# A four-layer hybrid decoder trunk: order of scores and values in the cross attention, the convolution's parameters on another queue, and later issue of norm scales and of the split memory

## The chip, the cores and the metric

The kernel runs on one core of one Trainium2 chip, as one program. The metric is the device time of that program in microseconds. Three runs of the kernel before gave 2044.0 to 2047.51 us, with a median of 2045.81. The profile shows one further execution, of 2043.62 us.

The core's engines each work through their own instructions in order: TensorE (PE in the profile, with PEld for its weight loads), VectorE (DVE), ScalarE (ACT), GpSimd (POOL) and SyncE (SP), which here only issues transfers. ScalarE and GpSimd have queues for transfers too, and an issue stands in line with their other instructions.

## The reference

The input is x of 256 tokens with 1024 features, and a memory of 256 tokens. There are four layers; each has a token mixer, a cross attention into the memory and an MLP. After each of these three the residual stream is normalized:

```python
for i in range(DEPTH):                     # 4 layers
    kind, j = i % N_MIXERS, i // N_MIXERS  # conv, dilated attention, RWKV-7, conv
    ...                                    # h = the token mixer of x
    x = layer_norm(DEEPNORM_ALPHA * x + h, ln_g[i, 0], ln_b[i, 0])
    h = memory_cross_attention(x, mem, x_w_q[i], x_w_kv[i], x_w_out[i])
    x = layer_norm(DEEPNORM_ALPHA * x + h, ln_g[i, 1], ln_b[i, 1])
    h = sq_relu_mlp(x, m_w1[i], m_w2[i])
    x = layer_norm(DEEPNORM_ALPHA * x + h, ln_g[i, 2], ln_b[i, 2])
```

The two parts that the change touches are these:

```python
def conv_module(x, w_in, b_in, dw, dw_b, ln_g, ln_b, w_out, b_out):
    h = x @ w_in + b_in
    val, gate = jnp.split(h, 2, axis=-1)
    h = val * jax.nn.sigmoid(gate)
    h = lax.conv_general_dilated(h, dw[:, None, :], ...) + dw_b   # causal, 31 taps, one filter a feature
    h = jax.nn.silu(layer_norm(h, ln_g, ln_b))
    return h @ w_out + b_out

def memory_cross_attention(x, mem, w_q, w_kv, w_out):             # 4 heads of 256
    q = (x @ w_q).reshape(b, s, XATTN_HEADS, XATTN_HEAD_DIM)
    kv = (mem @ w_kv).reshape(b, mem.shape[1], 2, XATTN_HEADS, XATTN_HEAD_DIM)
    p = jax.nn.softmax(jnp.einsum('bshe,bmhe->bhsm', q, kv[:, :, 0]) * (XATTN_HEAD_DIM ** -0.5), axis=-1)
    o = jnp.einsum('bhsm,bmhe->bshe', p, kv[:, :, 1])
    return o.reshape(b, s, D_MODEL) @ w_out
```

## The kernel before

**Products.** Every large product is computed from split operands: a matrix is a high part in a short format plus the low rest, and three matmuls (high by high, high by low, low by high) are summed in PSUM. Weights come in pieces of 128 x 1024 numbers (512 KB) through `chunk` (L131 to L141): SyncE issues the load into a staging tile `ws` (three buffers), ScalarE casts it to `wh` (L139), and an engine subtracts to get `wl` (L140; nine buffers each of `wh` and `wl`). That engine is VectorE in most of the kernel, and GpSimd (`lo_eng`) in the convolution's first part. A staging buffer is free when the subtraction has read it. x is transposed by TensorE and split in the same way into `xth` and `xtl` (`to_xt`, L153 and L154).

**Order.** The program is written as Python code that names the work; a scheduler with costs of its own then sets the order of each engine's instructions, near the order in which the code names them, and gives out the buffers. A transfer that is named late can therefore still be issued early, if its buffer is free and its queue has nothing else that can go.

**The convolution (layers 0 and 3).** `conv` loads the layer's norm scales (`load_gb`: `lng` and `lnb`, each a row spread to 128 partitions, 512 KB written), then the parameters (`conv_cols`): filter taps, biases and the inner norm's scales lie as rows, are loaded in three parts into one tile `craw` (one buffer, L465, L468, L470), transposed by TensorE (L471) and copied into `ccols` (L472). Then three tracks are merged by a table of due times: `glu` (eight units of 48 matmuls each, gate and value by turns, in PSUM tiles `psB` of which there are two), the taps on VectorE (L536), and the keys and values of the memory (`kv_unit`, units of 48 matmuls too). A gate unit ends in a sigmoid on ScalarE (L495), a value unit in an addition of its bias (L503); both read `ccols`.

**The memory.** In layer 0 `mem_t` loads the memory into `memrow` (which shares its buffer with `lng`), transposes and splits it into `mt`, and writes both parts to DRAM as `memd` (two writes of 1 MB, L305). Later layers read them back by GpSimd's queue (L297).

**The cross attention.** `xattn` computes q for 128 tokens at a time, in two banks of PSUM of 512 features, that is two heads, each (`first_rows`). A bank is copied (L381), transposed (L214) and copied into the four tiles of the heads (L384). `scores` of a head does eight fp32 matmuls on TensorE (four named ones of two passes, L346), the maximum on VectorE (L350, L351), the exponential on ScalarE (L355) and the division (L356, L359). `values` transposes the result, copies it by ScalarE (L366), multiplies it with the memory's values (L370) and splits the outcome into `oxt`. `project` then multiplies `oxt` with the output weights and normalizes. PSUM tiles `psA`, of which there are four, hold q's banks, the scores and the projection's sums.

Of the kernel before, what the change touches and what calls it, by code (L numbers as in the profile page):

```python
# [11 lines left out]
F32 = mybir.dt.float32  # L12
# [7 lines left out]
P = 128  # L20
# [64 lines left out]
class Trunk:  # L85
# [113 lines left out]
    def first_rows(self, xt, t, ws):  # L199


        out = [self.A(), self.A()]
        if t == 0:
            self.gemm_tok(xt, t, ws, out)
        else:
            for j in range(2):
                self.gemm_tok(xt, t, [[a[:, j * 512:(j + 1) * 512] for a in w] for w in ws], out[j:j + 1])
        return out
# [83 lines left out]
    def mem_t(self, tags=("xth", "xtl")):  # L292

        mt = [self.sb.tile([P, KC, S], F32R, name="mt", tag=g, bufs=2) for g in tags]
        if self.mem_d is not None:
            for a, d in zip(mt, self.mem_d):
                self.nc.gpsimd.dma_start(a, d)  # L297
            return mt
        for m in range(NT):
            mm = self.sb.tile([P, D], F32, name="memrow", tag="lng", bufs=1)  # L300
            self.nc.sync.dma_start(mm, self.t["mem"][0, m * P:(m + 1) * P, :])
            self.to_xt(mt, mm, m)
        self.mem_d = [self.dr.tile([P, KC, S], F32, name=f"memd{i}") for i in range(2)]
        for a, d in zip(mt, self.mem_d):
            self.nc.sync.dma_start(d, a.bitcast(F32))  # L305
        return mt
# [25 lines left out]
    def xattn(self, layer, kv, xt, xt_out):  # L332
# [52 lines left out]
        scores(0)  # L385
        scores(1)
        values(0)
        scores(2)
        values(1)
        scores(3)  # L390
# [64 lines left out]
    def conv_cols(self, j, cp):  # L455
# [3 lines left out]
        pt = self.T()  # L459
        dw = t_["a_dw"][j].rearrange("w (c p) -> (w c) p", p=P)  # L460
        for q in range(3):
            raw = cp.tile([P, P], F32, name="craw", tag="craw", bufs=1)
            if q < 2:
                n = 124
                nc.sync.dma_start(raw[:n, :], dw[q * n:(q + 1) * n, :])  # L465
            else:
                n = 40
                nc.sync.dma_start(raw[:16, :], t_["a_b_in"][j].rearrange("(c p) -> c p", p=P))  # L468
                for i, nm in enumerate(("a_dw_b", "a_ln_g", "a_ln_b")):
                    nc.sync.dma_start(raw[16 + 8 * i:24 + 8 * i, :], t_[nm][j].rearrange("(c p) -> c p", p=P))  # L470
# [6 lines left out]
    def conv(self, layer, j, xt, xt_out, fill):  # L477

        nc, v, t_ = self.nc, self.nc.vector, self.t
        gb = self.load_gb(layer, 0)  # L480
# [112 lines left out]
        self.lo_eng = v  # L593
        boh, bol = self.chunk(t_["a_b_out"][j:j + 1, :], None, rows=1)
# [712 lines left out]
def tile_trunk(ctx: ExitStack, tc: tile.TileContext, t: dict, out: bass.AP, stop: int = 99, layers=tuple(range(DEPTH))):  # L1307
# [12 lines left out]
    def memory(ls, tags):  # L1320
# [4 lines left out]
        return [lambda l=l, u=u: k.kv_unit(l, kv[l], u, mt) for l in ls for u in range(8)]  # L1325
# [94 lines left out]
```

## Time and profile before

| | |
|---|---|
| median of three runs | 2045.81 us |
| the profiled execution | 2043.62 us, its span 2041.9 us |
| TensorE busy | 1933.6 us, 95% of the span |
| VectorE, ScalarE, GpSimd busy | 1294.5, 994.7 and 270.4 us |
| transfers | 334.14 MB, 164 GB/s over the span |
| layer 0's convolution | from the start to about 184 us |
| the four cross attentions, from the end of q's last bank to the end of the values | 233 to 254, 799 to 819, 1366 to 1387 and 1801 to 1824 us |

Matmuls follow each other in a pipeline, so a record's duration (some 280 ns for 128 x 256) is longer than the time from one to the next (120 ns). Idle time of TensorE is therefore read from the stretches without any of its work, and the granted clock (1.00 or 0.50 in any short stretch) is looked at beside it.

### The profile page before, as it was taken

The numbers are of one execution on the slowest core, as the hardware profiler recorded it, in microseconds if no ns is written. First come the engines' busy times: TensorE is split into PE (matmuls) and PEld (weight loads), VectorE is DVE, ScalarE is ACT, GpSimd is POOL, SyncE is SP. The second block draws the span as 40 slices with busy tenths as digits, with TensorE's granted clock in tenths as the row PEclk, the third lists the DMA queues.
The fourth block names the chain that finished last, engine by engine and source line by source line (L and its number), as shares of the span: only waits on it lengthen the run. The fifth ranks groups of instructions, "written<-read, shape, count | busy, mean of one in ns | idle before, by whom it ended". The sixth has DMA issues, their size and how long they took to land.

```text
span 2041.9 us, 32951 instructions
## 1 busy us (share of the span) xinstructions
PE 1933.6 (95%) x12995; PEld 1708.8 (84%) x12995; DVE 1294.5 (63%) x2516; ACT 994.7 (49%) x1543; POOL 270.4 (13%) x168
## 2 busy tenths in 40 slices
PE   6999989999999998999999989989999898999998
PEld 6998779888999987798888777867898787878996
DVE  3896755546555566655496668776554599756544
ACT  4545536544545544365436544433655464545552
POOL 5870000000000000000021312100001653000000
PEclk8999999999999999999999889989999999999999
DMA  7644547667565645376645333553665532435762
GB/s 248 198 156 137 175 148 234 188 186 204 167 174 160 176 136 163 112 227 194 193 127 162 115 91 119 191 181 121 209 193 178 166 125 72 150 109 183 217 188 73
DMA packets 260604, 334.14 MB, mean 164 GB/s; under 512 B 25798, under 2 KB 220062, under 8 KB 259169
## 3 DMA queue, kind: packets, MB, share of 16 engines
q1 hardware_dynamic: 258144, 322.59, 51.2%
q0 software_dynamic: 1152, 8.39, 1.2%
q8 instruction: 102, 1.67, 0.3%
q10 hardware_dynamic: 1152, 1.05, 0.2%
q14 instruction: 54, 0.43, 0.1%
HBM read 321.96 MB, written 8.98 MB: 162 GB/s over the span
## 4 chain that ended last, share of the span: by engine, by line
PE 70%; DVE 14%; DMA 6%; ACT 4%; issue 4%; POOL 2%; SPq 0%; DVEq 0%; ACTq 0%; POOLq 0%
PE psA L172 25%; PE psB L184 19%; PE psB L196 7%; PE psB L655 6%; DVE g L536 3%; PE psT L214 3%; DVE wl L140 2%; ACT wh L139 2%; DMA ws<-in_m_w_dram 2%; POOL wl L140 2%; PE psB L370 1%; DVE bnst L271 1%; DVE x L270 1%; PE psA L196 1%; DMA ws<-in_a_w_in_dram 1%
## 5 line engine op out<-in xcount | busy, mean ns | idle before, releaser
L139 ACT CAST wh<-ws 128x1024 fp32r<-128x1024 f32 x546 | 572.2, 1052 | 668.0 <-PE psA L172 165.4
L140 DVE TENSOR_TENSOR wl<-ws,wh 128x1024 fp32r<-128x1024 f32 (+1 forms) x462 | 567.6, 1232 | 424.7 <-ACT wh L139 422.0
L184 PE MATMUL psB<-xth,wh 128*128 128x256 f32 x1152 | 332.7, 289 | 7.8 <-ACT xth L153 3.2
L184 PE MATMUL psB<-xth,wl 128*128 128x256 f32 x1152 | 330.4, 287 | 6.8 <-DVE wl L140 6.8
L184 PE MATMUL psB<-xtl,wh 128*128 128x256 f32 x1152 | 329.9, 286 | 0.0
L140 POOL TENSOR_TENSOR wl<-ws,wh 128x1024 fp32r<-128x1024 f32 x84 | 211.7, 2544 | 363.9 <-DMA ws<-in_a_w_in_dram 251.1
L184 PEld LDWEIGHTS psB<-xth,wh 128*128 128x128 f32 x1152 | 224.5, 195 | 12.4 <-ACT xth L153 3.8
L184 PEld LDWEIGHTS psB<-xth,wl 128*128 128x128 f32 x1152 | 224.2, 195 | 8.2 <-DVE wl L140 8.0
L184 PEld LDWEIGHTS psB<-xtl,wh 128*128 128x128 f32 x1152 | 224.6, 195 | 2.3 <-issue 0.2
L172 PE MATMUL psA<-wh,xth 128*128 128x512 f32 x496 | 180.6, 407 | 3.2 <-ACT xth L153 2.6
L172 PE MATMUL psA<-wl,xth 128*128 128x512 f32 x496 | 177.3, 401 | 0.0
L172 PE MATMUL psA<-wh,xtl 128*128 128x512 f32 x496 | 176.4, 400 | 0.0
L172 PE MATMUL psA<-wh,hth 128*128 128x512 f32 x512 | 163.7, 396 | 0.0
L172 PE MATMUL psA<-wh,htl 128*128 128x512 f32 x512 | 163.3, 395 | 0.0
L172 PE MATMUL psA<-wl,hth 128*128 128x512 f32 x512 | 162.3, 393 | 0.0
L536 DVE SCALAR_TENSOR_TENSOR psA<-chp,ccols,psA 128x256 f32<-128x256 f32 x280 | 119.6, 485 | 2.7
L172 PEld LDWEIGHTS psA<-wh,xth 128*128 128x128 f32 x496 | 95.2, 193 | 25.7 <-ACT xth L153 7.2
L172 PEld LDWEIGHTS psA<-wl,hth 128*128 128x128 f32 x512 | 96.5, 188 | 23.0
L172 PEld LDWEIGHTS psA<-wh,htl 128*128 128x128 f32 x512 | 96.2, 188 | 22.0
L172 PEld LDWEIGHTS psA<-wl,xth 128*128 128x128 f32 x496 | 95.4, 193 | 19.1
L172 PEld LDWEIGHTS psA<-wh,xtl 128*128 128x128 f32 x496 | 94.9, 192 | 19.1 <-DVE xtl L154 0.3
L655 PE MATMUL psB<-xth,wh 128*128 128x256 f32 x384 | 109.2, 284 | 1.0 <-ACT qk L660 1.0
(319 smaller groups left out, 3477.3 us busy)
## 6 DMA issues: line engine op xcount, KB each, us to landing
ws<-in_m_w_dram SPq DMA_DIRECT2D x256, 512.0 KB, 4.3
ws<-in_b_w_qkv_dram SPq DMA_DIRECT2D x72, 512.0 KB, 4.3
ws<-in_x_w_kv_dram SPq DMA_DIRECT2D x64, 512.0 KB, 3.5
ws<-in_a_w_in_dram SPq DMA_DIRECT2D x32, 512.0 KB, 4.2
ws<-in_x_w_q_dram SPq DMA_DIRECT2D x32, 512.0 KB, 4.6
ws<-in_x_w_out_dram SPq DMA_DIRECT2D x32, 512.0 KB, 4.5
ws<-in_c_w_rkv_dram SPq DMA_DIRECT2D x24, 512.0 KB, 3.6
ws<-in_a_w_out_dram SPq DMA_DIRECT2D x16, 512.0 KB, 4.3
```

The source lines that it names most:

```text
L139: nc.scalar.copy(out=h[:rows], in_=f[:rows])
L140: self.lo_eng.tensor_tensor(l[:rows], f[:rows], h.bitcast(F32)[:rows], op=OP.subtract)
L172: nc.tensor.matmul(ps[j], l, r[:, j * 512:(j + 1) * 512], start=first and k == 0 and i == 0, stop=last and k == n - 1 and i == 2)
L184: self.pe_last = nc.tensor.matmul(ps[:, c * S + toks.start:c * S + toks.stop], l, r, start=k == 0 and i == 0, stop=k == KC - 1 and i == 2).ins
L196: nc.tensor.matmul(ps[:, m * 256:(m + 1) * 256], l, r[:, k % 4, :], start=k == 0 and i == 0, stop=k == KC - 1 and i == 2)
L214: self.pe_last = self.nc.tensor.transpose(pt[:, i * P:(i + 1) * P], b, self.ident).ins
L270: v.scalar_tensor_tensor(xs, xs, ALPHA, ps[j], op0=OP.mult, op1=OP.add)
L271: v.bn_stats(st[:, j, :], xs)
L370: nc.tensor.matmul(op[:, c * S:(c + 1) * S], vt[:, m, (2 * h + c) * P:(2 * h + c + 1) * P], pT[:, m, :], start=m == 0, stop=m == 1)
L536: v.scalar_tensor_tensor(dst[:, o], hp[:, c, k:k + S], dwc(k, cc), src[:, o], op0=OP.mult, op1=OP.add)
L655: nc.tensor.matmul(ps, l[:, k, :], r[:, k, :], start=k == 0 and i == 0, stop=k == KC - 1 and i == 2)
```

## The change

1. In `xattn`, scores and values are named inside the loop over q's banks of the last 128 tokens: after the first bank scores of heads 0 and 1; after the second values of head 0, scores of head 2, values of head 1, scores of head 3. Before, all of these were named behind both banks. `first_rows` becomes a generator, so that the second bank's product is named after what is done with the first.
2. In `conv_cols` the three parts of the parameters go to three places of one 128 x 512 tile of the pool `g2`, and ScalarE issues their transfers.
3. In `conv` the norm scales are loaded (named) after the convolution, just before the output product.
4. The writes of the split memory become one item of work (`mem_keep`) in the middle of the sixteen units of keys and values.

```diff
@@ first_rows @@
-        out = [self.A(), self.A()]
         if t == 0:
+            out = [self.A(), self.A()]
             self.gemm_tok(xt, t, ws, out)
-        else:
-            for j in range(2):
-                self.gemm_tok(xt, t, [[a[:, j * 512:(j + 1) * 512] for a in w] for w in ws], out[j:j + 1])
-        return out
+            yield from out
+            return
+        for j in range(2):
+            ps = self.A()
+            self.gemm_tok(xt, t, [[a[:, j * 512:(j + 1) * 512] for a in w] for w in ws], [ps])
+            yield ps
@@ mem_t @@
+        return mt
+
+    def mem_keep(self, mt):
         self.mem_d = [self.dr.tile([P, KC, S], F32, name=f"memd{i}") for i in range(2)]
         for a, d in zip(mt, self.mem_d):
             self.nc.sync.dma_start(d, a.bitcast(F32))
-        return mt
@@ xattn @@
-        scores(0)
-        scores(1)
-        values(0)
-        scores(2)
-        values(1)
-        scores(3)
+                if t == NT - 1:
+                    for h in range(2):
+                        if i:
+                            values(h)
+                        scores(2 * i + h)
         values(2)
         values(3)
@@ conv_cols @@
+        raws = self.g2()
...
-            raw = cp.tile([P, P], F32, name="craw", tag="craw", bufs=1)
+            raw = raws[:, q * P:(q + 1) * P]
...
-                nc.sync.dma_start(raw[:n, :], dw[q * n:(q + 1) * n, :])
+                nc.scalar.dma_start(raw[:n, :], dw[q * n:(q + 1) * n, :])
...
@@ conv @@
-        gb = self.load_gb(layer, 0)
...
         self.lo_eng = v
+        gb = self.load_gb(layer, 0)
@@ memory @@
+        work = [lambda l=l, u=u: k.kv_unit(l, kv[l], u, mt) for l in ls for u in range(8)]
+        if k.mem_d is None:
+            work[len(work) // 2:0] = [lambda: k.mem_keep(mt)]
+        return work
```

Where this puts the instructions shows at three places. Line numbers of the kernel with the change are three to seven higher.

The first place is the start of SyncE's queue. Before:

```order
L301 DMA memrow<-in_mem_dram 128x1024
L258 DMA lnb<-in_ln_b_dram 128x1024
L465 DMA craw<-in_a_dw_dram 124x128
L138 DMA ws<-in_a_w_in_dram 128x4x256 x4
L301 DMA memrow<-in_mem_dram 128x1024
L138 DMA ws<-in_a_w_in_dram 128x4x256 x2
L257 DMA lng<-in_ln_g_dram 128x1024
L305 DMA memd_150<-mt 128x2048
L305 DMA memd_151<-mt 128x2048
L465 DMA craw<-in_a_dw_dram 124x128
L138 DMA ws<-in_a_w_in_dram 128x4x256 x2
L468 DMA craw<-in_a_b_in_dram 16x128
```

With the change:

```order
L303 DMA memrow<-in_mem_dram 128x1024
L138 DMA ws<-in_a_w_in_dram 128x4x256 x3
L260 DMA lnb<-in_ln_b_dram 128x1024
L138 DMA ws<-in_a_w_in_dram 128x4x256 x3
L303 DMA memrow<-in_mem_dram 128x1024
L138 DMA ws<-in_a_w_in_dram 128x4x256 x3
L310 DMA memd_1510<-mt 128x2048
L138 DMA ws<-in_a_w_in_dram 128x4x256 x3
L310 DMA memd_1511<-mt 128x2048
L138 DMA ws<-in_x_w_kv_dram 128x4x256 x2
L138 DMA ws<-in_a_w_in_dram 128x4x256
L259 DMA lng<-in_ln_g_dram 128x1024
```

The writes of the memory stand behind nine and twelve pieces of weights, before behind six; `lnb` stands behind three pieces, before ahead of all; `lng` moves from behind six pieces to behind fifteen; the parameters are gone from this queue.

The second place is the start of ScalarE (`mt` is the memory, `g` the sigmoid of the gate). Before:

```order
L106 CAST onesr<-ones 1x128
L153 CAST xth<-psT 128x4x128 x2
L139 CAST wh<-ws 128x1024
L153 CAST xth<-psT 128x4x128 x2
L139 CAST wh<-ws 128x1024
L153 CAST mt<-psT 128x4x128
L139 CAST wh<-ws 128x1024
L153 CAST mt<-psT 128x4x128
L139 CAST wh<-ws 128x1024
L153 CAST mt<-psT 128x4x128 x2
L139 CAST wh<-ws 128x1024 x4
L495 ACT_TABLE_LOAD
```

With the change, behind six issues of the parameters:

```order
L139 CAST wh<-ws 128x1024
L153 CAST xth<-psT 128x4x128 x2
L139 CAST wh<-ws 128x1024
L153 CAST xth<-psT 128x4x128
L139 CAST wh<-ws 128x1024
L153 CAST xth<-psT 128x4x128
L153 CAST mt<-psT 128x4x128 x2
L139 CAST wh<-ws 128x1024 x3
L153 CAST mt<-psT 128x4x128 x2
L139 CAST wh<-ws 128x1024 x2
L498 ACT_TABLE_LOAD
L498 ACTIVATE g_239<-psB,ccols 128x256 x2
```

The first cast of weights now stands ahead of the casts of x, and the fourth behind the first two of the memory; eight casts of weights stand ahead of the first sigmoid in both.

The third place is ScalarE in layer 1's cross attention, from the copy of q's first bank of the last tokens on (casts of `wh` are those of the output weights; `g<-psA,mx` are the exponentials of heads 0 to 3, `g<-psT` the copies for the values). Before:

```order
L381 COPY g_8319<-psA 128x512
L139 CAST wh<-ws 128x1024 x3
L381 COPY g_8328<-psA 128x512
L139 CAST wh<-ws 128x1024 x3
L355 ACTIVATE g_8346,den<-psA,mx 128x256 x2
L139 CAST wh<-ws 128x1024
L355 ACTIVATE g_8361,den<-psA,mx 128x256 x2
L139 CAST wh<-ws 128x1024
L366 COPY g_8372<-psT 128x512
L355 ACTIVATE g_8390,den<-psA,mx 128x256 x2
L153 CAST xth<-psB 128x512
L366 COPY g_8401<-psT 128x512
```

With the change:

```order
L385 COPY g_8292<-psA 128x512
L359 ACTIVATE g_8310,den<-psA,mx 128x256 x2
L359 ACTIVATE g_8325,den<-psA,mx 128x256 x2
L139 CAST wh<-ws 128x1024 x3
L385 COPY g_8356<-psA 128x512
L370 COPY g_8370<-psT 128x512
L139 CAST wh<-ws 128x1024 x2
L153 CAST xth<-psB 128x512
L139 CAST wh<-ws 128x1024 x2
L359 ACTIVATE g_8388,den<-psA,mx 128x256 x2
L370 COPY g_8399<-psT 128x512
L359 ACTIVATE g_8417,den<-psA,mx 128x256 x2
```

The exponentials of heads 0 and 1 now stand ahead of the second bank's copy, and seven casts of the output weights stand between them and those of head 2.

More of the change, by code (lines that the diff above doesn't have):

```diff
@@ L459, in conv_cols @@
         pt = self.T()
+        raws = self.g2()
         dw = t_["a_dw"][j].rearrange("w (c p) -> (w c) p", p=P)
         for q in range(3):
-            raw = cp.tile([P, P], F32, name="craw", tag="craw", bufs=1)
+            raw = raws[:, q * P:(q + 1) * P]
             if q < 2:
                 n = 124
-                nc.sync.dma_start(raw[:n, :], dw[q * n:(q + 1) * n, :])
+                nc.scalar.dma_start(raw[:n, :], dw[q * n:(q + 1) * n, :])
             else:
                 n = 40
-                nc.sync.dma_start(raw[:16, :], t_["a_b_in"][j].rearrange("(c p) -> c p", p=P))
+                nc.scalar.dma_start(raw[:16, :], t_["a_b_in"][j].rearrange("(c p) -> c p", p=P))
                 for i, nm in enumerate(("a_dw_b", "a_ln_g", "a_ln_b")):
-                    nc.sync.dma_start(raw[16 + 8 * i:24 + 8 * i, :], t_[nm][j].rearrange("(c p) -> c p", p=P))
+                    nc.scalar.dma_start(raw[16 + 8 * i:24 + 8 * i, :], t_[nm][j].rearrange("(c p) -> c p", p=P))
             nc.tensor.transpose(pt[:, q * P:q * P + n], raw[:n, :], self.ident[:n, :n])
@@ L1324, in memory @@
             kv[l] = k.kv_alloc()
-        return [lambda l=l, u=u: k.kv_unit(l, kv[l], u, mt) for l in ls for u in range(8)]
+        work = [lambda l=l, u=u: k.kv_unit(l, kv[l], u, mt) for l in ls for u in range(8)]
+        if k.mem_d is None:
+            work[len(work) // 2:0] = [lambda: k.mem_keep(mt)]
+        return work
     st = k.dr.tile([8, P, 512], F32, name="kvst")
```

## The prediction

> **What bounds the kernel now.** I read the page first, then busy time by stage, then the gaps of TensorE in the stages that the change touches.
>
> ```profile
> span 2041.9 us, 32951 instructions
> PE 1933.6 (95%) x12995; PEld 1708.8 (84%) x12995; DVE 1294.5 (63%) x2516; ACT 994.7 (49%) x1543; POOL 270.4 (13%) x168
> PE 70%; DVE 14%; DMA 6%; ACT 4%; issue 4%; POOL 2%; SPq 0%; DVEq 0%; ACTq 0%; POOLq 0%
> ```
>
> TensorE is busy 95% of the span and holds 70% of the chain that ended last. The amount of matmuls does not change, so the change can only win idle time of TensorE, or time in which its clock is halved: some 108 us of idle in all. Two places are touched. The first is the start; the view is busy time by stretch (TensorE busy, its weight loads, VectorE, ScalarE, GpSimd, granted clock, DMA share, GB/s).
>
> ```profile
> 19.40:29.98 10.58, 10.58 (x87) 10.10 (x85) 1.48 (x3) 3.08 (x4) 6.92 (x3) 1.00 0.94 329
> 29.98:39.73 9.75, 0.60 (x4) 0.32 (x3) 0.49 (x2) 4.27 (x6) 3.47 (x2) 0.66 0.57 197
> 39.73:43.30 3.57, 3.57 (x16) 3.57 (x17) 2.63 (x5) 2.65 (x4) 3.08 (x2) 0.50 0.75 236
> 43.30:70.36 27.06, 27.06 (x225) 26.84 (x224) 21.66 (x44) 13.36 (x17) 25.25 (x12) 1.00 0.64 203
> ```
>
> Between 29.98 and 39.73 TensorE does 0.60 us of work, and for 3.57 us after that its clock is at 0.50. The groups of that stretch and SyncE's queue say why.
>
> ```profile
> L471 PE MATMUL psT<-ident,craw 124*128 124x124 f32 (+1 forms) x2 | 0.6, 298 | 7.2 <-DMA craw<-in_a_ln_b_dram 4.3 <-DMA craw<-in_a_dw_dram 2.9
> L184 PE MATMUL psB<-xth,wh 128*128 128x256 f32 x1 | 0.6, 582 | 1.9 <-ACT g L495 1.9
> 22.80 1.16 SPq L305 DMA_DIRECT2D memd<-mt  x2
> 24.00 1.71 SPq L465 DMA_DIRECT2D craw<-in_a_dw_dram  x1
> 27.05 9.40 DMA ws<-in_a_w_in_dram
> ```
>
> The three parts of the conv parameters share one buffer, so part two was issued at 24.00, behind the two 1 MB writes of the split memory, and TensorE waited 2.9 us for it, 4.3 us for part three, and 1.9 us for the sigmoid that needs their transposes. A weight load issued behind the same writes took 9.40 us.
>
> The second place is the cross attention, between the end of q's last bank and the end of the values, in the four layers:
>
> ```profile
> 233.43:253.74 20.31, 18.55 (x92) 15.30 (x92) 15.07 (x32) 13.96 (x30) 0.00 (x0) 1.00 0.58 191
> 798.68:819.20 20.52, 18.08 (x90) 14.92 (x90) 14.76 (x32) 12.92 (x29) 0.00 (x0) 1.00 0.55 179
> 1366.32:1386.79 20.47, 18.08 (x90) 14.91 (x90) 14.76 (x32) 12.91 (x29) 0.00 (x0) 1.00 0.56 180
> 1801.37:1823.83 22.46, 19.90 (x92) 16.37 (x92) 15.16 (x32) 13.96 (x30) 0.00 (x0) 0.92 0.54 168
> 1811.40:1814.80 3.40, 2.91 (x9) 2.48 (x10) 3.25 (x8) 2.62 (x7) 0.00 (x0) 0.50 0.53 149
> ```
>
> Stretch less busy time gives TensorE's idle: 1.76, 2.44, 2.39 and 2.56 us, 9.15 together. In layer 3 the clock is also halved for 3.40 us, which costs half of that, 1.7.
>
> **Part A, the start.** What the third unit of weights (48 matmuls) waits for is the sigmoid of the first, which frees its PSUM bank. ScalarE works in order, and before and after the change eight casts stand ahead of that sigmoid.
>
> ```profile
> 11.03 1.05 ACT L139 CAST wh<-ws 128x1024 fp32r<-128x1024 f32 x1 [3.49 <-DMA ws<-in_a_w_in_dram]
> 37.54 1.28 ACT L495 ACT_TABLE_LOAD   x1
> 38.83 0.84 ACT L495 ACTIVATE g<-psB,ccols 128x256 f32<-128x256 f32 x2
> 40.28 1.06 ACT L139 CAST wh<-ws 128x1024 fp32r<-128x1024 f32 x1
> 69.68 1.05 ACT L139 CAST wh<-ws 128x1024 fp32r<-128x1024 f32 x1 [0.97 <-DMA ws<-in_x_w_kv_dram]
> 70.64 0.83 ACT L503 ACTIVATE chp<-psB,ccols 128x256 f32<-128x256 f32 x2
> 12.15 9.39 POOL L140 TENSOR_TENSOR wl<-ws,wh 128x1024 fp32r<-128x1024 f32 x4 [10.48 <-ACT wh L139]
> ws<-in_a_w_in_dram SPq DMA_DIRECT2D x32, 512.0 KB, 4.2
> 71.52 0.39 PE L184 MATMUL psB<-xth,wh 128*128 128x256 f32 x1 [1.16 <-ACT chp L503]
> ```
>
> Step 1: lnb (512 KB) now stands behind the first three weight pieces. At 329 GB/s that is 1.6 us; I take 1.3, so the first cast ends at 10.8 instead of 12.1. Step 2: there are three staging buffers, so the eighth piece can be issued when GpSimd has subtracted the fifth. A subtraction takes 2.35 us (9.39 / 4); five from 10.8 end at 22.6. The fourth cast now stands behind the memory's first casts on ScalarE, and these behind TensorE's still slow matmuls; I estimate 2.3 us for that: 24.9. Step 3: plus 4.2 for the load, 1.05 for the cast, 1.28 for the table and 0.84 for the sigmoid: 32.3, instead of 39.73. That is 7.4 us. The parameters themselves, issued by ScalarE in its first microseconds (it idles until its first cast of x, then 3.49 us more at 11.03) have over 15 us until TensorE reaches their transposes; the six issues cost nothing. In layer 3, where no such gap of TensorE is on record, they gain nothing. Step 4: the idle that remains there is about a microsecond, so the clock stays: 3.57 / 2 = 1.8 us. Step 5: at 71.52 TensorE waited 1.16 us for an activation that stands behind 21 casts; now 19 stand ahead of it. All three: 10.4 us.
>
> Against it: the two memory writes now stand behind the ninth and the twelfth piece, where TensorE should be working. At worst each costs the next load 9.40 - 4.2 = 5.2 us. The casts then run at (69.68 - 40.28) / 12 = 2.45 us each; the nineteenth ends at 30.2 + 11 x 2.45 = 57.2, and the eighth unit can start at 58.0 plus what the writes cost. TensorE alone would get there at 32.3 + 5 x 5.75 = 61.1 (48 matmuls at 27.06 / 225). So 3 us of writes are hidden; with 10.4 us the eighth unit starts at 68.4 and the gain is 3.1. Each write is issued one load ahead of the load that it delays, so I count half: 5.2 together, a start at 63.2, a loss of about 2. **A = -8.5 us, between -10.4 and -3.1.** After the eighth unit TensorE is dense, so it carries on to the end. The norm scales cost nothing at the stage's end: in the new order they still go out within the first 25 transfers.
>
> **Part B, the cross attention.** Layer 1, from the rows of its view:
>
> ```profile
> 799.41 6.64 PE L346 MATMUL psA<-kt,g 128*128 128x256 f32 x30
> 806.60 0.72 PE L214 MATMUL psT<-ident,g 128*128 128x128 f32 x4 [0.55 <-DVE g L359]
> 809.08 1.99 PE L370 MATMUL psB<-g,vt 128*128 128x256 f32 x8 [1.76 <-ACT g L366]
> 803.69 3.79 DMA ws<-in_m_w_dram
> 796.99 4.29 DMA ws<-in_x_w_out_dram
> 1799.94 5.04 DMA ws<-in_x_w_out_dram
> 278.88 7.42 DMA ws<-in_m_w_dram
> L297 POOL DMA_DIRECT2D mt<-memd x8: 530/568/699, 275.3 to 1323.2; - x8
> ws<-in_x_w_out_dram SPq DMA_DIRECT2D x32, 512.0 KB, 4.5
> ```
>
> Today TensorE runs out of work when it waits 0.55 us for VectorE's scaling of head 0, then 1.76 us for ScalarE's copy of its transpose, which had a cast and a weight load (803.69, 3.79 us) ahead of it. In the new order heads 0 and 1 go through their softmax under the 5.6 us of q's last bank, so both waits go. The next thing that is late is on ScalarE: the exponentials of heads 2 and 3, and in layers 1 and 2 the copy for values(1), stand behind the casts of the last pieces of the output weights. Call the end of q's last bank 0. TensorE has then: 2 scores (0.9; a score is two records of 0.22), two sets of transposes (1.2), 2 scores (0.9), values(0) (1.8), 1 score (0.4), transposes (0.6), 3 scores (1.3), 15 matmuls of the projection (3.5): values(1) is due at 10.6. ScalarE: the fifth piece can be issued when the second is subtracted, which VectorE does after the softmax of head 1, at about -1; it lands at 2.8, is cast (3.9) and subtracted (1.22, 5.1); then the eighth piece goes out, lands at 8.9, is cast (9.9); the exponentials of head 2 take 1.0 (10.9), the copy 0.6: 11.5. So TensorE waits 0.9 us with 3.79 per load and 1.9 with 4.29, since two loads stand in series; I take 1.3. In layers 0 and 3 head 2's exponentials stand ahead of those last casts and values(2) has seven more matmuls in front; the same count gives 1.0. New idle: 1.0 + 1.3 + 1.3 + 1.0 = 4.6 against 9.15, a gain of 4.5; and half of layer 3's clock loss, 0.9, because an idle under half as long should not always halve it. **B = -5.4 us.** Bounds: all of it gone, 9.15 + 1.7 = -10.9; with loads of 5.04 us each layer waits 1.4 more, which makes it about +0.2.
>
> On the clock, the Trainium skill (TensorE: Matmul & The Clock Gate, Part 1) says that the gate halves after at least one idle window of some 3.4 us. 29.98:39.73 and the 3.57 us after it agree; layer 3's halving after 2.56 us of idle in all does not. By that rule alone the 0.9 would be left out.
>
> **The sum.** A + B = -13.9 on the profiled execution's own 2043.62 us: 2029.7. The median of the runs before is 2045.81, 2.2 above that execution; on it the change gives 2031.9. I forecast 2031, between them.
>
> **Rivals.**
> 1. The memory writes starve GpSimd's subtractions: A falls to -3 or -5. For it: 40 to 70 us GpSimd is busy 25.25 of 27.06. Against it: 47 subtractions at 2.35 are 110 us, while TensorE needs 5.75 per two of them. Time: 2045.8 - 4 - 5 = 2037.
> 2. The casts before the exponentials eat B: loads of 5 us, B near 0. For it: 4.5 as median and 5.04 on the chain of layer 3. Time: 2045.8 - 8.5 = 2037.
> 3. Slower: the same place with loads as long as the one of 7.42 us. Two in series make each microsecond beyond 4.3 cost 2 us in each of four layers, 8 us; with B near -2 there and A at -8.5, it decides from 5.6 us a load, and at 7.42 the time is 2045.8 - 10.5 + 25 = 2060. Against it: that load was issued 3.6 us after GpSimd's read of the split memory (275.3), and no such read falls into the four stretches above.
> 4. It does nothing: the parameters land as late by the other queue, or the early idle goes to the weight loads. Time 2042 to 2047. Against it: they are issued some 15 us before use.
> 5. Both parts near their best: 2045.8 - 21 = 2025.
>
> **Numbers.** Forecast 0.55, rival 1 0.15, rival 2 0.09, rival 3 0.04, rival 4 0.06, rival 5 0.11. Range 2022 to 2039: from rival 5 with its runs' spread to both parts at the lower half of their bounds. A difference under 0.2%, about 4 us, can't be told from none here. So faster 0.90, same 0.06, slower 0.04.
>
> **What would show it.** Right: no idle of TensorE for the parameters, the third unit near 32 us at full clock, the eighth near 62; the memory written after 25 us; in each cross attention idle of about 1 us that ends on a copy for values(1) or values(2), with the casts of the output weights just ahead of it on ScalarE. Wrong: a wait for GpSimd or weight loads of 2 us and more between 40 and 70 us (A), exponentials of head 2 that start more than 2 us after their maximum (B), or VectorE's taps at the end of conv 0 as the new end of TensorE's waits.

## The result, and the profile after

The kernel before took 2046.66 us (median of six runs, 2043.27 to 2049.93), the changed kernel 2037.03 us (six runs, 2034.22 to 2039.25). The ratio is 0.9945, with a 95% interval of 0.9929 to 0.9962: faster by 9.6 us by the medians, by 11.3 us by the ratio, which is not the quotient of the two medians. A second series gave 0.9962 (0.9947 to 0.9977), with medians of 2040.60 and 2047.16. The forecast was 2031, its range 2022 to 2039: the direction and the range held, and the gain was about two thirds of the 14.8 us forecast.

The changed kernel's profile, its page first: span, TensorE's busy time, shares of the chain of waits.

```profile
span 2036.1 us, 32946 instructions
PE 1929.9 (95%) x12995; PEld 1703.0 (84%) x12995; DVE 1295.8 (64%) x2516; ACT 992.1 (49%) x1543; POOL 269.7 (13%) x168
PE 70%; DVE 13%; DMA 8%; ACT 4%; issue 3%; POOL 1%; SPq 0%; ACTq 0%; DVEq 0%; POOLq 0%
```

The shares hardly move; the change is read in its two stages. First the start, as busy time by stretch (TensorE, its weight loads, VectorE, ScalarE, GpSimd, granted clock, DMA share, GB/s). The kernel before:

```profile
12.50:45.00 32.50, 23.10 (x146) 21.84 (x147) 8.87 (x17) 15.14 (x21) 22.07 (x10) 0.74 0.69 233
45.00:80.00 35.00, 33.84 (x282) 33.63 (x281) 28.57 (x61) 17.64 (x23) 33.19 (x15) 1.00 0.66 209
80.00:110.00 30.00, 29.23 (x238) 28.52 (x236) 29.45 (x71) 16.65 (x25) 26.20 (x12) 1.00 0.61 194
```

The changed kernel:

```profile
12.50:45.00 32.50, 30.50 (x233) 29.33 (x234) 15.47 (x28) 17.73 (x24) 27.08 (x12) 1.00 0.79 268
45.00:80.00 35.00, 30.63 (x244) 30.02 (x243) 30.98 (x68) 18.02 (x23) 32.38 (x14) 0.97 0.67 215
80.00:110.00 30.00, 29.99 (x225) 28.57 (x224) 27.38 (x65) 18.06 (x30) 22.63 (x10) 0.98 0.60 193
```

Up to 45 us TensorE does 233 matmuls instead of 146, at full clock instead of 0.74. From 45 to 80 us it does 38 fewer than before: part of the lead goes back. Where, its own timeline shows (start, duration, and in brackets the idle before and what ended it):

```profile
31.74 0.39 PE L184 MATMUL psB<-xth,wh 128*128 128x256 f32 x1 [0.41 <-ACT g L498]
62.46 0.39 PE L184 MATMUL psB<-xth,wh 128*128 128x256 f32 x1 [1.67 <-ACT chp L506]
69.37 0.39 PE L184 MATMUL psB<-xth,wh 128*128 128x256 f32 x1 [0.89 <-ACT kt L327]
77.19 0.38 PE L184 MATMUL psB<-mt,wh 128*128 128x256 f32 x1 [1.81 <-ACT g L498]
```

The third unit starts at 31.74 and the eighth at 62.46, 9.06 us ahead of before's 71.52. Then come waits for ScalarE (0.89 and 1.81 us), and for 3.4 us from 78.1 on the clock is halved (0.97 and 0.98 in the stretches above). ScalarE's copy of q's first bank in layer 0, the first work of the cross attention that can be marked in every profile, starts at 217.7 us before (the first start in the row) and at 212.1 now:

```profile
L381 ACT COPY g<-psA x2: 590/592/595, 217.7 to 221.4; 128x512 f32<-128x512 f32 x2
```

```profile
L385 ACT COPY g<-psA x3: 585/587/593, 212.1 to 222.0; 128x512 f32<-128x512 f32 x3
```

Of the lead of 9 us some 5.6 is left in these two profiles. This mark is used below for all kernels.

Second, the cross attention, from that copy for the second half of the tokens to the end of the values, in the four layers. Before (stretch less TensorE's busy time is its idle time: 1.76, 2.44, 2.39, 2.56 us):

```profile
228.04:253.74 25.70, 23.94 (x118) 19.80 (x117) 18.57 (x35) 17.79 (x34) 0.00 (x0) 1.00 0.52 169
792.89:819.20 26.31, 23.87 (x118) 19.76 (x117) 18.26 (x35) 16.87 (x33) 0.00 (x0) 1.00 0.50 160
1360.52:1386.79 26.27, 23.88 (x118) 19.77 (x117) 18.26 (x35) 16.86 (x33) 0.00 (x0) 1.00 0.50 161
1795.98:1823.83 27.85, 25.29 (x118) 20.86 (x117) 18.66 (x35) 17.80 (x34) 0.00 (x0) 0.94 0.49 151
```

With the change (0.91, 0.62, 0.29, 0.66 us):

```profile
222.02:249.38 27.36, 26.45 (x130) 21.77 (x129) 18.66 (x35) 17.46 (x34) 0.00 (x0) 1.00 0.49 156
787.67:815.36 27.69, 27.07 (x129) 21.56 (x128) 18.72 (x35) 16.49 (x33) 0.00 (x0) 1.00 0.48 152
1359.15:1386.03 26.88, 26.59 (x129) 21.66 (x128) 18.72 (x35) 16.43 (x33) 0.00 (x0) 1.00 0.50 157
1792.68:1819.80 27.12, 26.46 (x130) 21.79 (x129) 18.61 (x35) 17.46 (x34) 0.00 (x0) 1.00 0.45 145
```

The stretches are as long as before, but hold 11 or 12 matmuls more, of the projection that follows; the idle fell from 9.15 to 2.48 us, and no clock is under 1.00. Behind them a wait grew. Layer 1's timeline, VectorE first and TensorE's transposes at the MLP's start behind it:

```profile
847.59 1.23 DVE L140 TENSOR_TENSOR wl<-ws,wh 128x1024 fp32r<-128x1024 f32 x1 [2.79 <-ACT wh L139]
...
848.97 1.42 DVE L279 SCALAR_TENSOR_TENSOR x<-x,bnrs,lnb 128x512 f32<-128x512 f32 x2
...
849.87 0.88 PE L216 MATMUL psT<-ident,x 128*128 128x128 f32 x3 [3.35 <-DVE x L279]
```

Before, this wait was 1.70 us:

```profile
853.74 1.29 PE L214 MATMUL psT<-ident,x 128*128 128x128 f32 x8 [1.70 <-DVE x L277]
```

The norm of the second half of the tokens stands on VectorE behind a subtraction for the MLP's weights whose load came late.

### The profile page after: what moved, and what is told of

Its sections match the earlier page's. It is cut to its first block, busy times and chain, and to the rows that moved or that the text cites. A ratio compares the mean times of both kernels' runs of the same rounds, so it can differ in the third digit from the quotient of the medians.

```text
span 2036.1 us, 32946 instructions
## 1 busy us (share of the span) xinstructions
PE 1929.9 (95%) x12995; PEld 1703.0 (84%) x12995; DVE 1295.8 (64%) x2516; ACT 992.1 (49%) x1543; POOL 269.7 (13%) x168
## 3 DMA queue, kind: packets, MB, share of 16 engines
q8 instruction: 102, 1.67, 0.3%
## 4 chain that ended last, share of the span: by engine, by line
PE 70%; DVE 13%; DMA 8%; ACT 4%; issue 3%; POOL 1%; SPq 0%; ACTq 0%; DVEq 0%; POOLq 0%
PE psA L172 25%; PE psB L184 20%; PE psB L659 6%; PE psB L196 6%; DVE g L539 3%; PE psT L216 3%; DVE wl L140 3%; ACT wh L139 2%; DMA ws<-in_m_w_dram 2%; DMA ws<-in_b_w_qkv_dram 2%; DMA ws<-in_x_w_out_dram 1%; PE psA L196 1%; DVE bnst L273 1%; DVE x L272 1%; PE psB L374 1%
```

## The experiments

Ratios are to the kernel before, run in turns on the same chip, with 95% intervals. The parameters alone and the two changes with six subtractions were measured on a second chip, the subtractions in the kernel before on a third, so rows of different chips are compared by their ratios alone. "Mark" is the first copy of q in layer 0, in microseconds of the profiled execution.

| kernel | ratio | interval | mark |
|---|---|---|---|
| before, first and second profile | 1 | | 217.7, 214.3 |
| the change, first and second series | 0.9945, 0.9962 | 0.9929–0.9962, 0.9947–0.9977 | 212.1, 213.9 |
| cross attention's order alone | 0.9970 | 0.9958–0.9981 | 216.8 |
| the start alone | 0.9977 | 0.9967–0.9987 | 212.9 |
| parameters by ScalarE's queue alone | 1.0011 | 1.0000–1.0022 | 218.2 |
| change, writes named as before (behind nine pieces) | 0.9943 | 0.9925–0.9962 | 214.7 |
| change, writes at 89 us | 0.9962 | 0.9948–0.9976 | 213.8 |
| change, writes behind 24 loads of x_w_kv | 0.9949 | 0.9932–0.9967 | 212.1 |
| change, six subtractions on VectorE | 0.9929 | 0.9912–0.9945 | 212.1 |
| the last two together | 0.9931 | 0.9917–0.9945 | 207.4 |
| before, six subtractions on VectorE | 0.9988 | 0.9976–0.9999 | 212.9 |
| change, MLP's first subtractions on GpSimd | 1.0029 | 1.0017–1.0041 | 212.4 |

**How far one profile can be trusted.** The kernel before and the change were run again.

> The kernel before once more, for a second profile: how far do the times of the stages of two executions of the same kernel lie apart? By the first one the stretch from the MLP's last unit of layer 1 to q's first bank of layer 2, which the change doesn't touch, was 1.0 to 3.7 us longer in every other profile. If that is scatter, this profile shows it too, and the stage differences of single profiles are good to some 2 us only.

The second profile of before has its mark at 214.3, 3.4 us ahead of the first, and the stretch between layers 1 and 2 is 1.4 us longer than in the first (2.62 against 1.19 us behind it). Its waits for the parameters were 2.6 and 3.1 us, where the prediction's profile had 2.9 and 4.3, and the third unit began at 37.94 instead of 39.73. So stages of single profiles are good to 2 or 3 us, and part A was worked out on an execution whose third unit began 1.8 us later than the other's.

> The changed kernel once more, on the same chip as the two others, as the kernel that they are compared with: 0.9945 times the kernel before, as measured, within 0.002; the idle behind the eighth unit (0.9 at 68.5 and 1.8 us at 75.4) and the waits of 2 to 3.4 us at the MLP's start in layers 1 and 3 show again if they belong to the order and not to one execution.

Its waits behind the eighth unit came back (0.86 at 68.5, 2.44 us at 75.4): they belong to the order. The second profile of the change starts the eighth unit at 62.47, that of before at 70.04: a lead of 7.57 us, of which 3.75 is left at the twelfth unit (89.46 against 93.21) and 0.4 at the mark. In the first pair it is 9.06, 4.36 (90.33 against 94.69) and 5.6. That about half goes between the eighth and the twelfth unit shows in both; what is left at the mark is within the scatter of single profiles. Of the waits at the MLP's start, layer 1's was smaller this time: TensorE's idle from the values' end to the MLP's third ReLU was 4.05 us there in the first profile and 2.51 us in the second, against 1.8 us before; layer 3's was 2.51 and 2.22.

**The two parts apart.** First the new order of scores and values alone, then the change with the old order:

```diff
-        scores(0)
-        scores(1)
-        values(0)
-        ...
+                if t == NT - 1:
+                    for h in range(2):
+                        if i:
+                            values(h)
+                        scores(2 * i + h)
```

> The kernel before with the new order of the cross attention alone. Theory 'passed on': in the changed kernel's profile the idle of TensorE inside the four cross attentions fell from 9.15 us to about 2 us, but the wait at the following MLP (transposes that wait for VectorE's norm of the second half of the tokens) grew from 1.70 to 3.35 us in layer 1, 5.07 to 6.21 in layer 0, 1.68 to 1.93 in layer 2, 1.76 to 2.29 in layer 3. So this order alone should win some 3 us (1 to 4). The prediction's step B said 5.4. Rival 2 of the prediction (casts ahead of the exponentials) says about 0, with waits of 2 us and more for the exponentials of heads 2 and 3 inside the cross attention.

> The changed kernel with the cross attention of the kernel before: only the start differs from before. The prediction's step A said 8.5 us. The changed kernel's profile puts the third unit at 31.74 us and the eighth at 62.46 us, as predicted, but new idle stands behind it (1.67 us at 60.8, 0.89 at 68.5, 1.81 at 75.4 and a halved clock from 78.1 to 81.5), which leaves about 5.5 us at the end of the first convolution. So by the profile 5 to 6 us here, and this and the cross attention alone add up to the change's 9.6 within 2 us. If the parts did not add up, something in the one would be hidden by the other.

The cross attention won 0.0030 of 2046 us, 6.1 us (3.9 to 8.6), the start 4.7 us (2.7 to 6.8). They add up to 10.8, within the two series of the change (11.3 and 7.8 by their ratios). So part B came in as predicted (5.4) or a little above, and what is missing is missing at the start: 4.7 instead of 8.5. My expectation of 3 us for the cross attention, read off single profiles of the whole, was too low.

**The parameters alone.** The kernel before with only these lines:

```diff
+        raws = self.g2()
-            raw = cp.tile([P, P], F32, name="craw", tag="craw", bufs=1)
+            raw = raws[:, q * P:(q + 1) * P]
-                nc.sync.dma_start(raw[:n, :], dw[q * n:(q + 1) * n, :])
+                nc.scalar.dma_start(raw[:n, :], dw[q * n:(q + 1) * n, :])
```

> The kernel before with the conv parameters by ScalarE's queue and in three buffers, and nothing else (memory writes behind seven weight pieces and the norm scales, as the order now puts them). It tells what the parameters alone are worth. If they are the whole of the start's gain: 3 to 5 us faster than before, as the start of the change alone (0.9977). If the norm scales' move is needed too: the third unit waits for the ninth weight piece behind the two writes until some 36 to 38 us, and the gain is under 2 us.

The waits for the parameters, 7.2 us before, are gone, and nothing is won. TensorE's waits from 13.5 to 112 us in that kernel (us in total, times, longest; a wait of 0.6 us is left out):

```profile
...
PE psB L184 <- ACT chp L504: 2.6, 2, 1.3
PE psT L214 <- DVE g L537: 1.9, 1, 1.9
PE psB L184 <- POOL wl L140: 1.9, 1, 1.9
PE psB L184 <- ACT g L496: 1.8, 1, 1.8
PE psB L184 <- ACT kt L323: 1.5, 2, 0.8
...
```

And ScalarE, where a weight load stands behind the norm scales and both memory writes:

```profile
37.70 1.05 ACT L139 CAST wh<-ws 128x1024 fp32r<-128x1024 f32 x1 [5.25 <-DMA ws<-in_a_w_in_dram]
```

Without the wait for the parameters TensorE runs into the next limit, the feed of weights (load, ScalarE's cast, GpSimd's subtraction), and pays 9.7 us in small waits up to 107 us, where the kernel before has 4.4 us beside its waits for the parameters. The feed had not moved: its eighth and nineteenth casts end at 38.75 and 66.38, in the two profiles of before at 37.52 and 67.34, and 35.73 and 64.10 (in the change at 29.53 and 61.67). So TensorE, whose third unit starts at 31.42 here, lost its lead again: the eighth unit starts at 64.12 (before 71.52 and 70.04), the twelfth at 92.90 (94.69 and 93.21). In the kernel before the feed used those 7 us. The Trainium skill (Trainium Kernel Development and Optimization, Key Constraints) says that transfers issued from several engines' queues run on the same DMA engines, and that another queue saves only issue time. This run is no test of it: the parameters did land in time here, since they have three places and no longer stand behind the two writes, and it is the feed that left nothing of it.

**The memory writes.** Three places for them. First named as before, right behind the split of the memory; in the queue they then stand behind nine pieces of weights, not six as in the kernel before, since the norm scales are later:

```diff
             self.to_xt(mt, mm, m)
+        self.mem_keep(mt)
         return mt
-        if k.mem_d is None:
-            work[len(work) // 2:0] = [lambda: k.mem_keep(mt)]
```

> The changed kernel with the memory writes at their old place, right behind the split of the memory (in SyncE's queue both behind the ninth weight piece, none later); parameters, norm scales and cross attention as changed. Theory 'price moves': the third unit starts some 3 to 5 us later than 31.7 us, the idle behind the eighth unit goes, and the time is the change's within 1.5 us. The prediction counted the writes at half price when placed midway (5.2 of 10.4 us); by that this kernel is some 3 to 5 us slower than the change.

The third unit starts at 31.9 us all the same, and the time is the change's (0.9943): the idle behind the eighth unit stayed (1.08, 1.47, 2.23 us between 68 and 85 us). So the expectation that the third unit would be late was wrong, and by time nothing shows of the half price that the prediction counted for writes placed midway. In the feed some of it does: the nineteenth cast ends at 63.10 here, at 61.67 in the change, and at 57.88 and 58.42 in the two kernels below whose writes come at 89 and 119 us. This part of the change is worth nothing that can be measured. Since the parameters alone won nothing and this kernel wins as much as the change, what the start needs beside the parameters is most likely the later norm scales, which in the kernel of the parameters alone stood, with the writes, ahead of the eighth piece. The norm scales' move was not run alone, so this is argued.

Later, held behind the last weight load issued so far in SyncE's queue (`ld_last`):

```diff
+        with self.tc.issue_after(self.ld_last):
             for a, d in zip(mt, self.mem_d):
                 self.nc.sync.dma_start(d, a.bitcast(F32))
```

> The changed kernel with the two writes of the split memory held behind sixteen more weight loads in SyncE's queue (20 of the kernel's loads of x_w_kv and a_w_in ahead of them instead of 9 and 12). Theory 'writes' (the prediction's rival 1): the two writes at 26.9 and 36.2 us delay the weight loads behind them, so that ScalarE's casts wait (3.37 us at 45.1) and TensorE's reads of PSUM with them; held, the idle at 60.8, 68.5 and 75.4 us and the halved clock at 78.1 go, and the kernel is 3 to 5 us faster than the change, some 2032 to 2034. Theory 'order': the idle comes from the place of ScalarE's PSUM reads behind casts that wait for GpSimd's subtractions at 2.35 us each; then the idle stays and the time is within 1.5 us of the change.

The waits at 68 and 75 us went; one of 1.30 us at 55.1 and one of 4.30 us at 101.3 came in their place. The stretches of this kernel around it:

```profile
90.00:95.00 5.00, 5.00 (x44) 5.00 (x43) 5.00 (x14) 1.99 (x3) 3.20 (x2) 1.00 1.02 359
95.00:101.30 6.30, 6.30 (x49) 5.89 (x47) 5.84 (x15) 1.43 (x3) 2.41 (x1) 1.00 1.01 363
101.30:105.60 4.30, 0.00 (x1) 0.00 (x1) 0.70 (x3) 3.78 (x8) 3.93 (x2) 0.78 0.14 40
```

For 11 us the DMA engines are full (share 1.01 and 1.02, some 360 GB/s), GpSimd is short of work (2 and 1 subtractions), a cast on ScalarE waits 4.87 us for its load, and TensorE stands still for a result of ScalarE that comes behind the casts: the price of 2 MB moved from one place to the other.

> The changed kernel with the two memory writes behind 24 of the 32 loads of x_w_kv, at some 125 us, where TensorE is dense and the changed kernel's DMA share is 0.2 to 0.55. Theory 'price moves': in the first 110 us the weights' stream has no slack, so 2 MB of writes cost some 4 us wherever they stand there (in the changed kernel as 0.89, 1.81 and a halved clock behind the eighth unit; with the writes at 89 us as one wait of 4.30 us at 101.3). At 125 us the stream is ahead, and the price goes: no wait over 1.5 us from 60 to 150 us, TensorE at the end of the first convolution some 4 us earlier than in the change, 3 to 4.5 us faster than the change. Theory 'always': the stream has no slack at 125 us either, a wait of 3 to 5 us shows between 130 and 150 us and the time is the change's within 1.5 us.

With eight more loads ahead of the writes (`work[12:0]` instead of the half), no wait over 0.7 us is left from 66 to 170 us; but 1.07 us at 55 and 2.86 us at 62 stand where the change had 1.67. Its ratio, 0.9949, is not apart from the change's: inconclusive by time.

**The feed itself.** In the changed kernel, on ScalarE, three casts of weights stand between one read of a PSUM bank and the next (L506, L327, L498 are the reads):

```profile
61.58 0.83 ACT L506 ACTIVATE chp<-psB,ccols 128x256 f32<-128x256 f32 x2
63.60 1.05 ACT L139 CAST wh<-ws 128x1024 fp32r<-128x1024 f32 x1 [1.19 <-DMA ws<-in_x_w_kv_dram]
65.31 1.05 ACT L139 CAST wh<-ws 128x1024 fp32r<-128x1024 f32 x1 [0.66 <-DMA ws<-in_x_w_kv_dram]
67.79 1.05 ACT L139 CAST wh<-ws 128x1024 fp32r<-128x1024 f32 x1 [1.43 <-DMA ws<-in_x_w_kv_dram]
68.74 0.58 ACT L327 COPY kt<-psB 128x512 f32<-128x512 f32 x1
70.65 1.05 ACT L139 CAST wh<-ws 128x1024 fp32r<-128x1024 f32 x1 [1.33 <-DMA ws<-in_x_w_kv_dram]
72.95 1.05 ACT L139 CAST wh<-ws 128x1024 fp32r<-128x1024 f32 x1 [1.25 <-DMA ws<-in_x_w_kv_dram]
75.36 1.05 ACT L139 CAST wh<-ws 128x1024 fp32r<-128x1024 f32 x1 [1.36 <-PE psB L184]
76.31 0.83 ACT L498 ACTIVATE g<-psB,ccols 128x256 f32<-128x256 f32 x2
```

From read to read it takes 7.16 and 7.57 us, where a unit of matmuls takes 5.75. The casts wait for loads (the load of the one at 75.36 landed at 75.26, as good as together with the matmul that the row names), and a load can only go out when GpSimd has subtracted a piece, at 18.98 / 8 = 2.37 us each without a break from 64.73 on:

```profile
64.73 18.98 POOL L140 TENSOR_TENSOR wl<-ws,wh 128x1024 fp32r<-128x1024 f32 x8 [0.59 <-ACT wh L139]
```

So six early pieces were given to VectorE, whose subtraction takes 1.22 us:

```diff
+        self.nch += 1
+        eng = nc.vector if self.nch in (3, 6, 9, 12, 15, 18) else self.lo_eng
-        self.lo_eng.tensor_tensor(l[:rows], f[:rows], h.bitcast(F32)[:rows], op=OP.subtract)
+        eng.tensor_tensor(l[:rows], f[:rows], h.bitcast(F32)[:rows], op=OP.subtract)
```

> The changed kernel with the low parts of the 3rd, 6th, 9th, 12th, 15th and 18th weight piece subtracted by VectorE instead of GpSimd. Theory 'feed': from 40 to 85 us GpSimd is busy without a break at 2.36 us a piece; ScalarE's reads of PSUM have up to three casts between them there, 3 x 2.4 = 7.2 us against 5.75 us of matmuls a unit, and this eats the lead of 9 us that TensorE has at the eighth unit. Six pieces fewer on GpSimd shorten its chain by up to 14 us, so the idle at 60.8, 68.5 and 75.4 us goes: 3 to 4.5 us faster than the change, first bank of q in layer 0 at some 208 us instead of 212 to 214. Theory 'taps': VectorE is 0.9 busy from 60 to 150 us, and six subtractions of 1.22 us push its taps 7 us back; the idle at 60 to 80 goes but comes back as waits for taps at 100 to 176 us, and the time is the change's within 1.5 us.

> The same six subtractions by VectorE, and the memory writes behind 24 of the 32 loads of x_w_kv. Theory 'feed': with neither GpSimd's chain nor the writes in the way no wait over 1 us is left from 30 to 150 us; 4 to 6 us faster than the change, some 2032 where before is 2046. Theory 'taps': as the run before it, within 1.5 us of the kernel with the late writes alone (0.9949 of before).

Alone it gave 0.9929, but in its profile the waits at 67.8 and 75.5 us stand as in the change (1.64 and 1.30 us) and the mark is at 212.1, so the profile does not show where that came from. Together with the late writes the mark is at 207.4, some 5 us ahead of the change, and the order on ScalarE is another: two casts between the reads.

```profile
61.98 0.83 ACT L510 ACTIVATE chp<-psB,ccols 128x256 f32<-128x256 f32 x2
62.82 1.05 ACT L140 CAST wh<-ws 128x1024 fp32r<-128x1024 f32 x1
66.74 1.05 ACT L140 CAST wh<-ws 128x1024 fp32r<-128x1024 f32 x1 [2.88 <-DMA ws<-in_x_w_kv_dram]
67.70 0.57 ACT L331 COPY kt<-psB 128x512 f32<-128x512 f32 x1
69.54 1.05 ACT L140 CAST wh<-ws 128x1024 fp32r<-128x1024 f32 x1 [1.26 <-DMA ws<-in_x_w_kv_dram]
71.84 1.06 ACT L140 CAST wh<-ws 128x1024 fp32r<-128x1024 f32 x1 [1.26 <-DMA ws<-in_x_w_kv_dram]
72.80 0.83 ACT L502 ACTIVATE g<-psB,ccols 128x256 f32<-128x256 f32 x2
```

5.72 and 5.10 us from read to read: TensorE is the limit again. What stays is a wait of 1.76 us at 61.1 and 3.4 us of half clock behind it (0.95 from 45 to 80 us). By 80 us the subtractions done are 23 and 24 in the two profiles of before, 22 with the parameters alone, 25 in the change, 26 here, and the marks stand in the same order; the kernel with writes at 89 us, though, also has 26, and its mark is at 213.8. Both kernels with the six subtractions are faster than before by more than the change measured in either of its series (2033.16 and 2032.80 us, against 2046.23); the intervals overlap that of the first series, so that they beat the change is likely, not certain.

> The kernel before with the low parts of the 3rd, 6th, 9th, 12th, 15th and 18th weight piece subtracted by VectorE, and nothing else. Theory 'two bounds side by side': in the kernel before the parameters' wait and the feed of weights end at nearly the same time, so that each alone is worth little (parameters alone: 1.0011 of before), and only both together bring the first bank of q 10 us forward; then this kernel is within 2 us of before. Theory 'feed first': the feed alone was the bound and the parameters' wait was hidden behind it; then this kernel is 4 us or more faster than before.

The feed alone wins 0.0012, 2.5 us (0.2 to 4.9), between the two theories' numbers and nearer to the first; its waits for the parameters are still there (3.4 and 3.1 us). Parameters alone: nothing. Together, with the late writes and norm scales: the difference between that kernel (0.9931) and the cross attention alone (0.9970) is about 8 us (4 to 12 by the two intervals, and measured on two chips). So the start had two limits side by side, the parameters with what stood ahead of the weights, and the feed; the share of the norm scales in the first is open.

**The MLP's start.** The subtractions of the MLP's first eight weight pieces on GpSimd, in layers 1 to 3:

```diff
+        self.lo_eng = nc.gpsimd if layer else nc.vector
         w1s = [self.chunk(w1[k * P:(k + 1) * P, :FU * 256], None) for k in range(KC)]
+        self.lo_eng = nc.vector
```

> The changed kernel with the low parts of the first eight weight pieces of the MLP subtracted by GpSimd instead of VectorE, in layers 1, 2 and 3. Theory 'VectorE': in layer 1 the DMA engines stand still from 834 to 838 us (share 0.04) since the three staging buffers wait for VectorE's subtractions, which stand between the splits and norms of the first half of the tokens, and the norm of the second half then stands behind a subtraction whose load came late (VectorE idle 2.79 us at 847.59). With the subtractions elsewhere the wait at the MLP's start shrinks by 1 to 2 us in each of three layers: 3 to 5 us faster than the change. Theory 'loads': a subtraction on GpSimd takes 2.35 us instead of 1.22, the staging buffers come free no earlier and the gain is nothing, or a loss of up to 3 us.

Slower, by more than either theory said: 1.0029 of before, where the change has 0.9945. TensorE's idle from the values' end to the third ReLU is 5.7, 5.7 and 5.9 us in these layers, against 4.1, 2.9 and 2.5 in the change: some 8 us more, about half of what the kernel lost against the change (0.0084 of 2046 us is 17 us). Where the rest went was not followed up. The first four subtractions in layer 1 take 11.20 / 4 = 2.80 us each, the next three 2.4:

```profile
828.41 11.20 POOL L140 TENSOR_TENSOR wl<-ws,wh 128x1024 fp32r<-128x1024 f32 x4 [12.68 <-DVE rs_a L241]
```

So the wait at the MLP's start is not a matter of VectorE's order alone: with slower subtractions, which also free the staging buffers later, it grows. A kernel with a fourth staging buffer was not tried.

## Why the prediction was right, and where not

**Part A, up to the eighth unit: right, and by its mechanism.** Predicted against the profile: first cast ends 10.8, 11.10; fifth subtraction 24.9, 24.08; third unit 32.3, 31.74; clock whole there, yes; nineteenth cast 57.2 plus what the writes cost (5.2 counted), 61.67; eighth unit 63.2, 62.46. With the writes at 89 and 119 us the nineteenth cast ends at 57.88 and 58.42, so the sum's 57.2 holds and the writes cost some 3.5 us of the 5.2 counted.

**Part A, "after the eighth unit TensorE is dense, so it carries on": the step that failed.** The lead of 9.06 us at the eighth unit shrank to about 5.6 at the mark in that profile, and to 4.7 us in time when the start is changed alone. In the kernel before TensorE was dense there because it was late: the feed had used the wait. The sum compared the feed with TensorE at one point, the eighth unit, and took the rate behind it from TensorE. What the runs show in its place are waits of 0.89 and 1.81 us and a halved clock: from the eighth unit's start to the twelfth's it is 27.9 and 27.0 us in the two profiles of the change, 23.2 in both of before. The feed's mean rate would not have told: the two pieces of a unit take 2 x 2.37 = 4.7 us, less than the 5.75 of its matmuls. It is the order on ScalarE, with three casts that wait for pieces ahead of two reads in a row, that makes it 7.16 and 7.57 us. So the sum should have gone on unit by unit, with the casts that stand ahead of each read, until the feed was ahead by its buffers.

**Rival 1** (the memory writes starve GpSimd's subtractions, 2037) named the right engine and, by number, the right time. Its mechanism is half of it: writes named at their old place cost no more, at 89 us they cost a wait there instead, and only in the kernel with GpSimd relieved and the writes late does the profile keep the lead. **Rival 4** (the early idle goes to the weight loads) is what the parameters alone do, 1.0011.

**The size of the parameters' wait** was read from one execution; in the second profile of before the third unit starts 1.8 us earlier. That the six issues on ScalarE cost nothing holds for the third unit, but the first was later: the cast of weights now stands ahead of x's casts, TensorE stood 5.41 us at 7 us (before: 0.55 and 3.24 us), and its first product of weights began at 14.16 instead of 12.61.

**Part B: right in size, by other terms.** Over five profiles with the old order and eight with the new (that with the MLP's subtractions on GpSimd left out), from q's first copy of the second tokens to the MLP's third ReLU: TensorE's idle inside the cross attentions fell from a mean of 9.6 to 3.2 us (6.4, where 4.5 was predicted), the idle behind them rose from 11.1 to 13.6 us, and the four stretches together were 6.3 us shorter (287.7 to 281.4). The kernel with this order alone measured 6.1. What is left, 6.3 - 6.4 + 2.4 = 2.3 us, is the clock: taken as half of TensorE's busy time in halved stretches, it cost a mean of 8.8 us with the old order and 4.5 with the new, 4.3 less, while TensorE's other busy time there grew by 1.9 us, for a reason not looked into. In the two profiles of before four of the eight cross attentions had a granted clock of 0.94, in the two of the change and in that of the order alone none of twelve. The 0.9 counted for it was too low. So B came out near in part by luck: 1.9 us more idle inside and 3.4 us more clock than counted were won, and 2.4 and 1.9 us lost that were not counted. What would be late next was named as the copies for values(1) and values(2), with idle of about 1 us there. That sign did not come: no wait of the change's two profiles in these stretches ends on such a copy. The idle of 0.3 to 0.9 us sits mainly at the projection's first matmuls, which wait for ScalarE's cast of the values' outcome in layers 0 and 3 (0.75 and 0.51 us in the first profile) and for an exponential in layers 1 and 2 (0.29 each). And the larger wait, at the MLP's start, was not foreseen. Rivals 2 and 3 did not come, though the change's cross attentions have loads of the output weights of 4.6 to 5.6 us: of the two in series only the first was long (5.39, then 3.17 us in layer 1). ScalarE's copy for values(1) was done there 11.2 us after q's last bank, near the sum's 11.5; but TensorE, with more work in front than counted, came to it at 11.6 and not at 10.6, and did not wait.

**The sum.** -13.9 predicted, -10.8 by the two parts alone, -9.6 by the medians: A is 3.8 short (4.7 instead of 8.5), which is its lead behind the eighth unit, part of it the long wait in the profile used; B is 0.7 above its 5.4. And much of the gain is clock. Over the whole span TensorE's idle went from 108.3 and 109.4 us in the two profiles of before to 106.2 and 103.7, while the half clock cost 37.4 and 39.3 us before and 29.6 and 33.6 now.

## What to carry to other kernels

When a long wait of the main engine is removed, ask what used that time to get ahead: here the feed of weights did, and the parameters moved alone won nothing, the feed relieved alone 2.5 us, both (with norm scales and writes later) about 8. Carry a lead on unit by unit, by what stands ahead of each step in the new order, until the feed is ahead by its buffers, instead of by the rate of the engine that happens to be dense in the old profile. And take a second profile of the unchanged kernel before a term of the sum rests on one wait's length: here the start of the third unit differed by 1.8 us.

## What was not expected of the hardware

With idle of 1.8 to 3.0 us in a stretch of some 27 us the granted clock was halved in four of eight cross attentions; with 0.3 to 0.9 us in none of twelve. The Trainium skill (TensorE: Matmul & The Clock Gate, Part 1) names at least one idle window of some 3.4 us, freely running; these idles are shorter and in several pieces, and still halve it at times. The traces say when: in each of the fourteen profiles the halvings begin on a grid of 3.41 us, and of their 56 cross attentions 13 were halved, each right behind a stretch of that grid with 1.67 to 2.42 us of idle. Of the 43 others, 40 had at most 1.61 us in any such stretch, and three 1.72 to 1.87. So in these stages idle of about half a grid stretch went ahead of a halving, not a whole idle stretch, and idle cut in pieces over two stretches went free (2.44 us in all, at most 1.18 in one, in layer 1 of the first profile of before). A subtraction of 128 x 1024 on GpSimd took 2.37 us beside VectorE's taps and 2.80 us in layer 1's MLP start when it was moved there; what slowed it there was not looked into. And the first weight load, issued by SyncE at 3.10 us before, went out at 4.90 with the parameters' six small transfers ahead on ScalarE's queue; that these hold it is only argued.
